# A two-layer sequence encoder on one core: which low parts a DMA forms, a fourth form of x made a chunk sooner, and one add from two neighbouring banks

## The chip, the cores and the metric

The kernel runs on one core of a Trainium2 chip. The metric is the device time of one execution in microseconds (us), lower is better. The core's engines run side by side and meet at semaphores: TensorE (PE in the profile, PEld for its loading of stationary operands), VectorE (DVE), ScalarE (ACT), GpSimd (POOL), SyncE (SP), and DMA queues that SP, POOL and ACT issue to. TensorE writes its products to PSUM, eight banks of 128 partitions x 512 floats; VectorE and ScalarE read them there.

## The reference

Two layers over 512 frames of width 1024, float32. Each layer has two half-step SwiGLU feed-forwards around a mixer (an mLSTM in layer 0, a gMLP in layer 1), then a gated input embedding, and each residual ends in a LayerNorm:

```python
def swiglu_ffn(x, w_gu, w_d):                     # hidden width 2816
    g, u = jnp.split(x @ w_gu, 2, axis=-1)
    return (jax.nn.silu(g) * u) @ w_d

for i in range(2):
    x = layer_norm(alpha*x + 0.5*swiglu_ffn(x, ffn1_wgu[i], ffn1_wd[i]), ...)
    x = layer_norm(alpha*x + mixer_i(x), ...)     # mLSTM (i = 0), gMLP (i = 1)
    x = layer_norm(alpha*x + 0.5*swiglu_ffn(x, ffn2_wgu[i], ffn2_wd[i]), ...)
    x = layer_norm(alpha*x + sigmoid(x @ ple_wg[i] + ple_bg[i]) * (p[i] @ ple_wp[i]), ...)
```

The change touches the feed-forwards. There are four of them; they are called first to fourth below, in order of time.

## The kernel before, in words

**Two parts for one number.** Each operand of a product is split into a high part (a copy in a rounded format, ScalarE) and a low part (what the copy lost). `mm3` multiplies high by high, high by low and low by high, so a block costs three matmuls (L353, L354, L355). The low part of a weight is formed by VectorE as source minus high part (L251, or L257 where it is put off), or by ScalarE and a DMA: ScalarE writes the source times -1 as rounded (L248), and a DMA that POOL issues adds the source to it (L249).

**The weights' queue.** `Weights` keeps one list of everything that has to be split, in the order of use. `fill` goes down that list as long as slots are free (four `main` slots for most, two `rows` slots for the down products), `take` hands out the next pair of parts, `release` gives a slot back when its product is issued and fills again. Raw weights come by SP's queue into three buffers of 1 MB (`load`, L208); a buffer is used again when every part formed from it is done.

**Seven products for eight.** Blocks of a matrix product are computed as two by two blocks in seven products instead of eight, with sums formed beforehand. For the up projection (gate and value columns of the weights, `up_forms`) the weight sums are formed in place in the raw tiles: product 2's operand in a quarter of g (L141, L142), product 4's there again (L149, L150). Products are counted from 0; `UP_BY_DMA` lists those whose low part is formed by DMA, and so marked as formed as soon as the DMA is issued (`done`). Others, in these chunks, are put off (`apart`): their subtraction runs at the next `lows()`, and only then does the product count as formed. `form_ahead(3)` forms the sums of the next three entries ahead of their turn if what they need is formed.

**A feed-forward** (`ffn`) goes through the 22 hidden blocks in six chunks of 2, 4, 4, 4, 4, 4. Chunks 0 to 3 compute the hidden activations block by block (`up`, tile `fps`). Chunks 4 and 5 (`up_products`) compute two blocks, a pair, by seven products (`UpPair`, tile `ups`, right operands from `UpForms`), so 14 products to a chunk and two pairs. While chunk c computes its hidden blocks, the down projection of chunk c-1 runs between them, again by seven products (`Group`, tile `gps`); after each, `add` adds the result to x in SBUF. The last chunk's down projection is done by `down` at the end (tile `dps`), block of 128 rows by block, followed by the LayerNorm.

**x's forms.** `UpForms` computes the sums of x that stand to the right in the pair's products. Its `steps` are run two at a time in chunk 3, from product `FORM_AT` on; what must wait for chunk 4 (one form is written over x's own parts) stands in `last` and runs behind the given product of chunk 4. The seventh product of the first pair needs the fourth form, high part L1003 and low part L1008.

**Banks.** Four PSUM banks belong to the up products (`up_bank`), four to everything else (`dn_bank`): down products, x's transposes (`turn_x`, run by hooks while the first products of the next stage go on), the mixers' smaller products. `dn_bank` takes the bank that has been free longest. A group holds two banks for its even and two for its odd products; `unpin` gives them back after its last two adds, L727. `add` issues one VectorE instruction for each bank.

**What sets the order.** The program is written out by hand: each engine executes its instructions in the order in which the Python code issues them, and waits in that order.

Of the kernel before, what the change touches and what calls it, by code (L numbers as in the profile page):

```python
# [10 lines left out]
F32 = mybir.dt.float32  # L11
F32R = mybir.dt.float32r
AF = mybir.ActivationFunctionType
# [31 lines left out]
PLE_EXTRA = 3  # L45
UP_BY_DMA = (1, 2, 4)

# [275 lines left out]
def hybrid_trunk(ctx: ExitStack, tc, x, p, ln_g, ln_b, ffn1_wgu, ffn1_wd, ffn2_wgu, ffn2_wd,  # L323
# [20 lines left out]
    ps_up = ctx.enter_context(tc.tile_pool(name="ps_up", bufs=1, space=PSUM))  # L344
    ps_dn = ctx.enter_context(tc.tile_pool(name="ps_dn", bufs=1, space=PSUM))
    dram = ctx.enter_context(tc.tile_pool(name="dram", bufs=1, space=DRAM))
# [33 lines left out]

    dn_order, pinned = deque(range(4)), {}

    def dn_bank(name, pin=False):

        i = next(i for i in dn_order if i not in pinned.values())
        dn_order.remove(i)
        dn_order.append(i)
        bank = ps_dn.tile([P, 512], F32, name=name, tag=f"dn{i}")
        if pin:
            pinned[id(bank)] = i  # L390
        return bank

    def unpin(bank):
        i = pinned.pop(id(bank))
        dn_order.remove(i)
        dn_order.append(i)
# [40 lines left out]
    UP_FROM = 4  # L437
    FORM_AT = 3
    turn_p = []
# [424 lines left out]
    class Group:  # L864
# [58 lines left out]
        def product(self):  # L923
            r = self.next_product
            self.next_product += 1
            if len(self.ready) == 1:
                self.finish_form()
            w, f = W.take(), self.ready.popleft()
            if r < 2:
                self.banks.append([dn_bank("gps", True) for _ in range(2)])  # L930
            for e, ps in enumerate(self.banks[r % 2]):
                for k in range(self.half):
                    i, j = (e, k) if self.by_tokens else (k, e)
                    mm3(ps, [a[:, i, j * P:(j + 1) * P] for a in f], [a[:, k] for a in w],
                        k == 0 and r in (0, 1, 3), k == self.half - 1, r not in (0, 1, 3))

        def add(self):

            r = self.next_add
            if r == self.next_product:  # L940
                return
            self.next_add += 1
            i, j = self.TO[r]
            for e, ps in enumerate(self.banks[r % 2]):
                residual(2 * i + e, j, ps, r in self.first)
                if r >= 5:
                    unpin(ps)


    class UpForms:  # L950


        def __init__(self, pool, late):
# [37 lines left out]

            def t3_t2():
                split(*self.t3, b)
                vec.tensor_sub(f32r(self.t2, late, "wlo"), c, self.t2[0].bitcast(F32))

            def x21():
                for i, s in enumerate(halves):
                    joined(d[i], 1, 0, s)

            def t4():  # L1000
                for i, s in enumerate(halves):
                    vec.tensor_sub(d[i], d[i], c[:, s])
                    sca.activation(f32r(self.t4, pool, "f1")[:, s] if not i else self.t4[0][:, s], d[i], AF.Copy)  # L1003

# [4 lines left out]

            self.last = {0: t3_t2, 2: x21, 3: t4, 4: t4_low}  # L1010
            self.right = [self.quarter(0, 0), self.quarter(1, 0), self.t2, self.t1, self.t3,
# [57 lines left out]
    def ffn(layer, k, rows, late, prepare=None):  # L1069
        with stage_pool("forms", 2) as fpool, stage_pool("quarters", Q_BUFS) as qpool, \  # L1070
                stage_pool("hpool", 2) as hpool, stage_pool("tforms") as tpool:
            name = (layer, k)
            W.open_raw(name, qpool, Q_BUFS)
            banks = deque(up_staged((layer, k) == (0, 0)))

# [48 lines left out]
            for c, n in enumerate(FFN_CHUNKS):  # L1124
# [52 lines left out]
                if c == 0:  # L1177
                    run_affine()
            W.apart = False
            return down(hs, False, norm, lazy=layer == 0, defer=prepare is not None)  # L1180

# [675 lines left out]
    def warm(n):  # L1857

        ps = up_bank("warm")
        for _ in range(n):  # L1860
            nc.tensor.transpose(ps[:, :P], ident, ident)

    warm(16)
    turn_x(0)
# [14 lines left out]
    gmlp()  # L1879
    ffn_ple(1, True)  # L1880


# [25 lines left out]
```

## Time and profile before

| | us |
|---|---|
| time, median of 3 runs | 2288.68 (2285.99 to 2288.74) |
| time of the profiled execution | 2286.79 |
| its span, first to last instruction | 2285.1 |
| TensorE busy | 2214.1 (97%) |
| VectorE busy | 1711.5 (75%) |
| ScalarE busy | 1049.7 (46%) |
| GpSimd busy | 145.4 (6%) |
| granted TensorE clock, mean | 0.985 |

The four stages with `up_products` lie at about 213 to 349, 983 to 1121, 1409 to 1546 and 2052 to 2192 us. The profile tells for each engine how long it was busy, and for idle time what ended it (the releaser, named by engine, tile and line). Line numbers are those of the code above. A tile's name stands without its number; `x2` at the end of a timeline row means two instructions in a row. "PEclk" is the share of full clock speed that TensorE was granted.

### The profile page before, as it was taken

To read this page: it belongs to the slowest core of one execution; us is meant where nothing else is said; L and a number is where in the kernel's file an instruction comes from. 1 tells how busy PE (TensorE), PEld (TensorE's weight loads), DVE (VectorE), ACT (ScalarE), POOL (GpSimd) and SP (SyncE) were. 2 spreads that over 40 slices of the span, in tenths; PEclk is the share of its full clock that TensorE was granted. 3 is DMA by queue.
4 is the path that set the end of the run, shared out by engine and by line. 5 is a ranking of instruction groups with operands and counts; after the bars stand their busy time and mean duration, and the time that the engine had idled before them with its cause. 6 is when DMAs were issued, how large, how long until landed. Compare 5 with 4: busy or idle time off the path is not lost.

```text
span 2285.1 us, 29387 instructions
## 1 busy us (share of the span) xinstructions
PE 2214.1 (97%) x11669; PEld 1908.1 (84%) x11669; DVE 1711.5 (75%) x2468; ACT 1049.7 (46%) x1476; POOL 145.4 (6%) x183
## 2 busy tenths in 40 slices
PE   9999889999999999989899999889999999998898
PEld 8888888888888888889788888887888888888887
DVE  5668887776776776788786768777788767688887
ACT  4335556464646533355354335545345453345532
POOL 1000000111101000000000000000011100000000
PEclk9999999999999999999999999999999999999999
DMA  6324543466747443335432324543438733344441
GB/s 200 104 87 127 150 118 122 103 152 128 163 111 148 127 141 101 100 95 148 129 124 86 117 78 123 146 127 114 138 75 158 174 102 111 102 120 133 104 142 56
DMA packets 213233, 278.91 MB, mean 122 GB/s; under 512 B 6580, under 2 KB 161332, under 8 KB 213096
## 3 DMA queue, kind: packets, MB, share of 16 engines
q1 hardware_dynamic: 168080, 211.83, 28.8%
q0 software_dynamic: 38400, 50.52, 14.1%
q10 hardware_dynamic: 6616, 14.69, 2.0%
q8 instruction: 92, 1.51, 0.3%
q14 instruction: 45, 0.37, 0.1%
HBM read 224.58 MB, written 2.11 MB: 99 GB/s over the span
## 4 chain that ended last, share of the span: by engine, by line
PE 84%; DVE 9%; ACT 2%; DMA 2%; issue 2%; DVEq 0%; ACTq 0%; POOL 0%; POOLq 0%
PE fps L353 8%; PE fps L355 8%; PE fps L354 8%; PE gps L355 6%; PE gps L353 6%; PE gps L354 6%; DVE wlo L257 3%; PE ups L354 2%; PE ups L353 2%; PE ups L355 2%; PE dps L354 2%; PE dps L353 2%; PE dps L355 2%; DMA wlo<-wraw 2%; PE gups L353 1%
## 5 line engine op out<-in xcount | busy, mean ns | idle before, releaser
L242 ACT ACTIVATE whi<-wraw 128x1024 fp32r<-128x1024 f32 (+1 forms) x388 | 400.5, 1048 | 206.9 <-DVE wraw L142 64.3
L353 PE MATMUL fps<-xh,whi 128*128 128x512 f32 x800 | 311.4, 389 | 0.0
L354 PE MATMUL fps<-xl,whi 128*128 128x512 f32 x800 | 311.3, 389 | 0.0
L355 PE MATMUL fps<-xh,wlo 128*128 128x512 f32 x800 | 311.2, 389 | 0.0
L251 DVE TENSOR_TENSOR wlo<-wraw,whi 128x1024 fp32r<-128x1024 f32 (+1 forms) x210 | 252.4, 1217 | 48.0 <-ACT whi L242 47.2
L353 PE MATMUL gps<-whi,fhi 128*128 128x512 f32 x644 | 251.9, 391 | 0.0
L354 PE MATMUL gps<-wlo,fhi 128*128 128x512 f32 x644 | 251.6, 391 | 0.0
L355 PE MATMUL gps<-whi,flo 128*128 128x512 f32 x644 | 251.3, 390 | 0.0
L242 ACT ACTIVATE whi<-wquarter 128x1024 fp32r<-128x1024 f32 (+1 forms) x140 | 136.0, 971 | 221.5 <-PE gps L355 141.4
L251 DVE TENSOR_TENSOR wlo<-wquarter,whi 128x1024 fp32r<-128x1024 f32 (+1 forms) x92 | 97.7, 1062 | 160.8 <-ACT whi L242 160.8
L249 POOL DMA_DIRECT2D wlo<-wraw x96 | 100.7, 1049 | 1515.9 <-ACT wlo L248 1328.0
L727 DVE TENSOR_TENSOR xt<-xt,gps 128x512 f32<-128x512 f32 x302 | 193.9, 682 | 3.1 <-PE gps L355 2.8
L355 PEld LDWEIGHTS fps<-xh,wlo 128*128 128x128 f32 x800 | 150.1, 188 | 31.2
L353 PEld LDWEIGHTS fps<-xh,whi 128*128 128x128 f32 x800 | 150.2, 188 | 31.1
L354 PEld LDWEIGHTS fps<-xl,whi 128*128 128x128 f32 x800 | 150.2, 188 | 31.1
L353 PE MATMUL ups<-xh,whi 128*128 128x256 f32 x512 | 145.2, 284 | 0.0
L354 PE MATMUL ups<-xl,whi 128*128 128x256 f32 x512 | 145.0, 283 | 0.0
L355 PE MATMUL ups<-xh,wlo 128*128 128x256 f32 x512 | 145.0, 283 | 0.0
L355 PEld LDWEIGHTS gps<-whi,flo 128*128 128x128 f32 x644 | 120.9, 188 | 26.2
L905 ACT ACTIVATE fhi<-h 128x512 fp32r<-128x512 f32 (+1 forms) x140 | 81.0, 579 | 131.6 <-DVE h L1149 47.5
L353 PEld LDWEIGHTS gps<-whi,fhi 128*128 128x128 f32 x644 | 121.2, 188 | 23.9
L354 PEld LDWEIGHTS gps<-wlo,fhi 128*128 128x128 f32 x644 | 121.1, 188 | 23.7
(361 smaller groups left out, 5104.7 us busy)
## 6 DMA issues: line engine op xcount, KB each, us to landing
wraw<-in_ffn_wgu_dram SPq DMA_DIRECT2D x79, 1024.0 KB, 7.1
wlo<-wraw POOLq DMA_DIRECT2D x96, 512.0 KB, 5.2
wquarter<-in_ffn_wd_dram SPq DMA_DIRECT2D x64, 512.0 KB, 3.8
wraw<-in_ml_w_in_dram SPq DMA_DIRECT2D x24, 1024.0 KB, 5.6
wraw<-in_gm_w_in_dram SPq DMA_DIRECT2D x15, 1024.0 KB, 5.5
wraw<-in_ffn_wgu_dram SPq DMA_DIRECT2D x17, 512.0 KB, 5.0
wraw<-in_ffn_wd_dram SPq DMA_DIRECT2D x8, 1024.0 KB, 5.0
wraw<-in_ml_w_out_dram SPq DMA_DIRECT2D x8, 1024.0 KB, 4.9
```

Source lines behind the costliest of these rows:

```text
L242: self.nc.scalar.activation(hi[:, s], src[:, s], AF.Copy)
L249: self.nc.gpsimd.dma_start(lo[:, s], src[:, s], accum_op=OP.add)
L251: self.nc.vector.tensor_sub(lo[:, s], src[:, s], hi[:, s].bitcast(F32))
L257: self.nc.vector.tensor_sub(lo, src, hi.bitcast(F32))
L353: mm(ps, st[0], mv[0], start=start, stop=False, skip_group_check=more)
L354: mm(ps, st[0], mv[1], start=False, stop=False, skip_group_check=more)
L355: mm(ps, st[1], mv[0], start=False, stop=stop, skip_group_check=more)
L727: vec.tensor_add(dst, dst, ps)
L905: sca.activation(hi, src, AF.Copy)
```

## The change

It has three parts.

1. `UP_BY_DMA` becomes (1, 4, 5, 6): the low parts of a pair's weights for products 1, 4, 5 and 6 are formed by ScalarE and DMA, that of product 2 by VectorE.
2. `FORM_AT` becomes 2, and the sum for x's fourth form and its high part (`x21`, `t4`) move from chunk 4 to the steps of chunk 3; the low part runs behind product 3 of chunk 4 instead of product 4.
3. In the feed-forwards the four banks form two tiles of two neighbouring banks (`use_dn(2)`), and `add` adds both at once, 1024 numbers a partition. Before `down`, and outside the feed-forwards, there are four tiles of one bank (`use_dn(1)`). Each `use_dn` starts the order of the tiles anew from the first. A user of a single bank (`dn_bank`) in a feed-forward takes the first half of a tile of two.

```diff
-UP_BY_DMA = (1, 2, 4)
+UP_BY_DMA = (1, 4, 5, 6)
...
-    dn_order, pinned = deque(range(4)), {}
-
-    def dn_bank(name, pin=False):
+    dn_order, pinned, dn = deque(), {}, {}
+
+    def use_dn(width):
+
+        if dn:
+            assert not pinned
+            dn["context"].__exit__(None, None, None)
+        dn["context"] = tc.tile_pool(name=f"ps_dn{width}", bufs=1, space=PSUM, reuse_waits="tile")
+        dn["pool"], dn["width"] = dn["context"].__enter__(), width
+        dn_order.clear()
+        dn_order.extend(range(4 // width))
+
+    def dn_tile(name, pin=False):
 
         i = next(i for i in dn_order if i not in pinned.values())
         dn_order.remove(i)
         dn_order.append(i)
-        bank = ps_dn.tile([P, 512], F32, name=name, tag=f"dn{i}")
+        tile_i = dn["pool"].tile([P, dn["width"], 512], F32, name=name, tag=f"dn{i}")
         if pin:
-            pinned[id(bank)] = i
-        return bank
+            pinned[id(tile_i)] = i
+        return tile_i
+
+    def dn_bank(name):
+        return dn_tile(name)[:, 0]
...
-    FORM_AT = 3
+    FORM_AT = 2
...  (Group.product)
             if r < 2:
-                self.banks.append([dn_bank("gps", True) for _ in range(2)])
-            for e, ps in enumerate(self.banks[r % 2]):
+                self.banks.append([dn_tile("gps", True) for _ in range(2 // dn["width"])])
+            for e in range(2):
+                tiles = self.banks[r % 2]
+                ps = tiles[0][:, e] if len(tiles) == 1 else tiles[e][:, 0]
...  (Group.add)
-            for e, ps in enumerate(self.banks[r % 2]):
-                residual(2 * i + e, j, ps, r in self.first)
+            tiles = self.banks[r % 2]
+            for e, ps in enumerate(tiles):
+                n = 2 // len(tiles)
+                dst = xt[:, 2 * i + e:2 * i + e + n, j * 512:(j + 1) * 512]
+                if r in self.first:
+                    vec.scalar_tensor_tensor(dst, dst, ALPHA, ps, op0=OP.mult, op1=OP.add)
+                else:
+                    vec.tensor_add(dst, dst, ps)
                 if r >= 5:
                     unpin(ps)
...  (UpForms)
+            def x21():
+                for i, s in enumerate(halves):
+                    joined(d[i], 1, 0, s)
+
+            def t4():
+                hi = f32r(self.t4, pool, "f1")
+                for i, s in enumerate(halves):
+                    vec.tensor_sub(d[i], d[i], c[:, s])
+                    sca.activation(hi[:, s], d[i], AF.Copy)
...
-            self.last = {0: t3_t2, 2: x21, 3: t4, 4: t4_low}
+            self.steps += [x21, t4]
+            self.last = {0: t3_t2, 3: t4_low}
...  (ffn, ahead of its first product)
+            use_dn(2)
             banks = deque(up_staged((layer, k) == (0, 0)))
...  (ffn, at its end)
             W.apart = False
+            use_dn(1)
             return down(hs, False, norm, lazy=layer == 0, defer=prepare is not None)
```

`use_dn(1)` is also called once at the very beginning.

More of the change, by code (lines that the diff above doesn't have):

```diff
@@ L344, in hybrid_trunk @@
     ps_up = ctx.enter_context(tc.tile_pool(name="ps_up", bufs=1, space=PSUM))
-    ps_dn = ctx.enter_context(tc.tile_pool(name="ps_dn", bufs=1, space=PSUM))
     dram = ctx.enter_context(tc.tile_pool(name="dram", bufs=1, space=DRAM))
@@ L387, in dn_bank, with unpin @@
         dn_order.append(i)
-        bank = ps_dn.tile([P, 512], F32, name=name, tag=f"dn{i}")
+        tile_i = dn["pool"].tile([P, dn["width"], 512], F32, name=name, tag=f"dn{i}")
         if pin:
-            pinned[id(bank)] = i
-        return bank
-    def unpin(bank):
-        i = pinned.pop(id(bank))
+            pinned[id(tile_i)] = i
+        return tile_i
+    def dn_bank(name):
+        return dn_tile(name)[:, 0]
+    def unpin(tile_i):
+        i = pinned.pop(id(tile_i))
         dn_order.remove(i)
@@ L990, in __init__ @@
             d = [tmp.tile([P, 2, 256], F32, name="x_d", tag="pad", bufs=3) for _ in range(2)]
-            def t3_t2():
-                split(*self.t3, b)
-                vec.tensor_sub(f32r(self.t2, late, "wlo"), c, self.t2[0].bitcast(F32))
             def x21():
@@ L1000, in t4, with t3_t2 @@
             def t4():
+                hi = f32r(self.t4, pool, "f1")
                 for i, s in enumerate(halves):
                     vec.tensor_sub(d[i], d[i], c[:, s])
-                    sca.activation(f32r(self.t4, pool, "f1")[:, s] if not i else self.t4[0][:, s], d[i], AF.Copy)
+                    sca.activation(hi[:, s], d[i], AF.Copy)
+            def t3_t2():
+                split(*self.t3, b)
+                vec.tensor_sub(f32r(self.t2, late, "wlo"), c, self.t2[0].bitcast(F32))
             def t4_low():
@@ L1861, in warm @@
             nc.tensor.transpose(ps[:, :P], ident, ident)
+    use_dn(1)
     warm(16)
@@ L1880, in hybrid_trunk @@
     ffn_ple(1, True)
+    dn["context"].__exit__(None, None, None)
 _INS = ['x', 'p', 'ln_g', 'ln_b', 'ffn1_wgu', 'ffn1_wd', 'ffn2_wgu', 'ffn2_wd',
```

## The prediction

> **What bounds the kernel now.** I read the busy times first, then TensorE's own list of waits, then the granted clock behind the longest waits, and last the timelines of VectorE, ScalarE and TensorE around them.
>
> ```profile
> span 2285.1 us, 29387 instructions
> PE 2214.1 (97%) x11669; PEld 1908.1 (84%) x11669; DVE 1711.5 (75%) x2468; ACT 1049.7 (46%) x1476; POOL 145.4 (6%) x183
> ```
>
> TensorE is busy 97% of the span; 71.0 us are left idle. Whatever else the change does to the other engines, it can give back only that idle time and what the clock loses behind it. The waits of TensorE say where it lies:
>
> ```profile
> PE ups L353 <- ACT us L1045: 28.4, 4, 8.1
> PE ups L354 <- DVE t_f L1008: 23.1, 4, 5.8
> PE dps L353 <- DVE xt L727: 4.3, 2, 2.2
> ```
>
> 51.5 us of it stand in two rows, four waits in each: one of either kind in every feed-forward, all in the stage with the products of pairs (`up_products`). Call them A (L1008, the low part of x's fourth form, 5.8 us each) and B (L1045, the first copy of a pair's bank, 6.6 to 8.1 us). Behind each the clock is down; the rows are six-microsecond stretches that begin where the eight waits end, the granted clock being the third figure from the right (0.65, 0.73, ...):
>
> ```profile
> 245.20:251.20 6.00, 6.00 (x34) 6.00 (x35) 4.64 (x5) 2.94 (x4) 0.64 (x1) 0.65 0.49 127
> 324.70:330.70 6.00, 5.98 (x31) 5.69 (x32) 6.00 (x8) 6.00 (x8) 0.85 (x1) 0.73 0.45 86
> 1015.50:1021.50 6.00, 6.00 (x30) 6.00 (x31) 4.63 (x5) 2.95 (x4) 0.65 (x1) 0.56 0.51 127
> 1095.70:1101.70 6.00, 6.00 (x31) 5.74 (x32) 6.00 (x8) 6.00 (x8) 0.84 (x1) 0.70 0.47 90
> 1441.50:1447.50 6.00, 5.97 (x28) 5.97 (x29) 4.67 (x5) 2.91 (x4) 0.61 (x1) 0.50 0.48 126
> 1521.70:1527.70 6.00, 6.00 (x30) 5.79 (x31) 6.00 (x8) 5.73 (x8) 0.84 (x1) 0.64 0.46 87
> 2084.50:2090.50 6.00, 5.99 (x33) 5.99 (x34) 4.65 (x5) 2.93 (x4) 0.63 (x1) 0.61 0.48 125
> 2165.80:2171.80 6.00, 6.00 (x28) 5.88 (x29) 6.00 (x8) 5.25 (x8) 0.86 (x1) 0.56 0.46 87
> ```
>
> The shortfalls 0.35, 0.27, 0.44, 0.30, 0.50, 0.36, 0.39 and 0.44 of 6 us sum to 18.3 us, 2.3 us a wait. So A and B together cost 51.5 + 18.3 = 69.8 us.
>
> Why they are there, in the first feed-forward (start, duration, engine and line; idle time before it in brackets):
>
> ```profile
> 231.11 1.29 DVE L964 TENSOR_TENSOR x_d<-xh,xl 128x512 f32<-128x512 f32 x2
> 235.85 1.29 DVE L1002 TENSOR_TENSOR x_d<-x_d,x_f 128x512 f32<-128x512 f32 x2
> 244.46 1.29 DVE L1008 TENSOR_TENSOR t_f<-x_d,t_f 128x512 fp32r<-128x512 f32 x2
> 255.17 1.23 DVE L150 TENSOR_TENSOR wraw<-wraw 128x1024 f32<-128x1024 f32 x1 [5.30 <-DMA wlo<-wraw]
> 317.56 1.23 DVE L150 TENSOR_TENSOR wraw<-wraw 128x1024 f32<-128x1024 f32 x1 [5.32 <-DMA wlo<-wraw]
> 319.90 0.69 DVE L1064 SCALAR_TENSOR_TENSOR us<-us 128x512 f32<-128x512 f32 x1
> 324.09 0.58 ACT L1045 ACTIVATE us<-ups 128x512 f32<-128x512 f32 x1
> 324.72 0.58 PE L353 MATMUL ups<-t_whi,whi 128*128 128x256 f32 x1 [6.75 <-ACT us L1045]
> ```
>
> ```profile
> 211.00:235.00 24.00, 24.00 (x171) 22.59 (x170) 22.27 (x26) 11.06 (x14) 0.83 (x1) 1.00 0.35 85
> DVE wraw L150 <- DMA wlo<-wraw: 54.5, 12, 5.4
> ```
>
> Wait A: VectorE (third busy figure: 22.27 of 24 us) is behind, and the low part at 244.46 stands in its queue after everything else of that stretch. Wait B: L150 overwrites the quarter of the weights that the DMA of product 2's low part still reads (products count from 0), and VectorE stands still for it, 5.3 us at a time, 54.5 us in twelve places. Then `gated` (L1064) is late, ScalarE's splits of it are late, and the copy of the next pair's bank, queued behind them on ScalarE, releases TensorE at 324.7.
>
> **The change part by part.**
>
> *Low parts of products 1, 4, 5, 6 by DMA instead of 1, 2, 4.* Sixteen pairs. Product 2's low part comes onto VectorE, those of 5 and 6 leave it: 16 subtractions fewer there, 16 more scaled copies on ScalarE, 16 more issues on POOL. What matters is the order: L150 now follows a VectorE instruction of its own queue, so the 54.5 us of standing still go. As product 2 counts as formed only when its low part has run, L149 and L150 are issued one product later, behind `gated`.
>
> ```profile
> 1122.18 6.90 DVE L257 TENSOR_TENSOR wlo<-wraw,whi 128x1024 fp32r<-128x1024 f32 x6 [1.30 <-ACT whi L242]
> 303.53 1.04 ACT L248 ACTIVATE wlo<-wraw 128x1024 fp32r<-128x1024 f32 x1
> wraw<-in_ffn_wgu_dram SPq DMA_DIRECT2D x79, 1024.0 KB, 7.1
> DMA to landing us min/median/max: 4.5/5.2/14.3
> ```
>
> A low part is 6.90/6 = 1.15 us. Wait B: without the 5.3 us and the low parts of products 5 and 6 (2.3 us), L1064 comes by 312.3 instead of 319.9; from there to the end of L1045 it is 4.8 us, 317.1; TensorE wants the bank at 324.72 - 6.75 = 318.0. With L149 and L150 (2.4 us) behind `gated` as well, some 3 us are to spare: B goes. The product that needs L150's result has 11.5 us of work ahead of its weights (4 to L150's end, two passes of ScalarE 2.0, 0.3 to POOL, 5.2 landing); TensorE has four products of 24 matmuls and two down products of 12 before it, 120 x 24/171 = 16.8 us by the row of 171 matmuls in 24 us.
>
> For the low parts now by DMA the path from a freed slot is 2.0 + 0.3 + 5.2 = 7.5 us; until use there are three products and two down products, 96 matmuls, 13.5 us. So they land 6.0 us early: cost 0 under that cover. On SP the next pair's load of 1 MB (7.1 us) is now behind product 5's DMA instead of a VectorE instruction, and lands about 14.6 us after the slot came free, 2.8 us after VectorE reaches L141 (84 matmuls, 11.8 us); the bank's copies and adds queued behind it on VectorE have a few us of slack. POOL's queue holds nothing but these issues there; ScalarE, 46% busy, hides its copies. For all of this I put 3 us (nothing at one end, and one of the two waits staying, 36.6 us for B with its clock, at the other); the lower end is nearer, as the covers above are.
>
> *x's fourth form a chunk sooner.* `FORM_AT` 2 instead of 3 moves every step one product sooner; L964's pair (1.29 us), L1002's pair (1.29) and the fourth form's high part on ScalarE go into the chunk before, to the place that the splits of t1 leave, and its low part one product sooner, to where L1002 stood. It issues no DMA. Without these 2.6 us and two low parts it starts at about 235.85 - 1.29 - 2.3 = 232.3; TensorE needs it at 245.2 - 5.8 = 239.4. A goes, with 7 us to spare.
>
> *One add from two banks.*
>
> ```profile
> L727 DVE TENSOR_TENSOR xt<-xt,gps 128x512 f32<-128x512 f32 x302 | 193.9, 682 | 3.1 <-PE gps L355 2.8
> ```
>
> The feed-forwards' 280 adds of 0.68 us become 140 of twice the size: one start saved each, next to nothing (two in a row last 1.28 us in the rows below, one instruction over 1024 numbers 1.23, as L150). VectorE is off the path there, so 0.
>
> *The banks.* This speaks against the change. `use_dn` starts the order anew, and two banks are now one tile. In a feed-forward the five groups take the two tiles in turns; four hooks before them (an even number) leave the order as it was, so in the second, third and fourth the last group's seventh product sits in tile 0. In the first, a fifth use (`colps`) shifts it to tile 1. `use_dn(1)` then gives the closing `down` banks 0 and 1, which are tile 0: its first row block must wait for the last add, while before it took the banks free longest and only the second block met that add.
>
> ```profile
> 1128.99 1.28 DVE L727 TENSOR_TENSOR xt<-xt,gps 128x512 f32<-128x512 f32 x2
> 1128.92 0.39 PE L353 MATMUL dps<-whi,wquarter 128*128 128x512 f32 x1
> 1130.28 0.39 PE L353 MATMUL dps<-whi,wquarter 128*128 128x512 f32 x1
> 1553.28 1.28 DVE L727 TENSOR_TENSOR xt<-xt,gps 128x512 f32<-128x512 f32 x2
> 1554.02 0.50 PE L353 MATMUL dps<-whi,wquarter 128*128 128x512 f32 x1 [2.16 <-DVE xt L727]
> 2199.83 1.28 DVE L727 TENSOR_TENSOR xt<-xt,gps 128x512 f32<-128x512 f32 x2
> 2201.30 0.39 PE L353 MATMUL dps<-whi,wquarter 128*128 128x512 f32 x1
> ```
>
> The add is late by itself (it is behind five or six low parts on VectorE, the row at 1122.18, which wait for slots that the last product frees), so a faster VectorE does not help. The second block starts at 1130.28, 1554.02 and 2201.30 now. Then the first block would start at the add's end (1130.2, 1554.5, 2201.0), run 24 matmuls of (1130.28 - 1128.92)/6 = 0.227 us, 5.4 us, and lose 2.3 us of clock as after the eight waits: second block at 1137.9, 1562.2, 2208.7. That is 7.6 + 8.2 + 7.4 = 23.2 us more.
>
> Entering a feed-forward, the hooks that turn x take tile 0 and then tile 1:
>
> ```profile
> 782.89 0.60 PE L595 MATMUL xps<-ident,xt 128*128 128x128 f32 x4
> 783.81 0.67 DVE L727 TENSOR_TENSOR xt<-xt,dps 128x512 f32<-128x512 f32 x1
> 1849.46 0.60 PE L595 MATMUL xps<-ident,xt 128*128 128x128 f32 x4
> 1852.76 0.67 DVE L727 TENSOR_TENSOR xt<-xt,dps 128x512 f32<-128x512 f32 x1
> ```
>
> In the second feed-forward the second hook (782.89) must now wait for the mixer's last add (784.48): 1.6 us. In the fourth, the gMLP's `down` ends in banks 0 and 1 (its single banks are taken in multiples of four but for the two of the last spatial product), so the first hook (1849.46) waits until 1853.43: 4.0 us, and between 0 and 2.3 of clock, of which I take 1. Together 6.6.
>
> **Sum:** -51.5 - 18.3 + 23.2 + 6.6 + 3 = -37.0 us. Against the profiled span 2285.1 that is 2248; that execution's time, 2286.79, stands 1.9 below the median 2288.68, so the median becomes 2251.
>
> The Trainium skill, "TensorE: Matmul & The Clock Gate", Part 1, "What's actually happening", says that the clock halves after an idle window and comes back after one busy window of about 3.4 us. By that a long wait would cost 1.7 us of clock; with eight waits gone and three come the estimate from the page is 2255. The rows behind the waits (2.3 us each) decide for the sum above.
>
> **The rivals.**
>
> *No bank waits.* If the tiles lie otherwise than I read them, the 29.8 us of the last two parts do not come: 2222. For it: the whole of them is argued from the order of the code; against it: the order can be followed step by step.
>
> *One wait stays in part.* VectorE, standing at L141 for the load that is now behind a DMA, may keep `gated` late. B whole would give 2251 + 36.6 - 3 = 2285, half of it about 2268. For it: the load's 7.1 us begin only when a DMA has landed; against it: 3 us of margin for B, 7 for A.
>
> *Slower: weights late by DMA.* TensorE waits for no low part by DMA now. Four of seven go that way after, three in consecutive products (4, 5, 6), beside SP's loads. A landing takes 4.5 to 14.3 us; above 13.5 - 2.3 = 11.2 us TensorE waits, and above 12.4 us (1.2 us more at each of the 32 products) the gain is gone. At 14.3 us it would be 32 x 3.1 = 99 us, 2350. Against it: the landing that VectorE waited for at L150, in the chain of waits, took 4.51 us from its issue.
>
> ```profile
> 312.93 4.51 DMA wlo<-wraw
> ```
>
> The Trainium skill, "DMA: Bandwidth & Descriptors", "Issuing engines are not separate DMA queues", says that transfers from SP and POOL run on the same 16 engines and interleave, which is how this would come about; the median row, 5.2 us, does not bear out so much of it.
>
> **How the numbers follow.** The forecast, 2251 (2240 to 2262 by the bounds of clock and loads), 0.56; no bank waits 0.15; a wait that stays 0.20, of which 0.04 near 2285; late weights 0.09. The range 2218 to 2276 leaves out the last case and the upper end of the third, 0.16. About 0.2%, 4.6 us, is what a measurement can tell: faster 0.56 + 0.15 + 0.16 = 0.87, same 0.04, slower 0.09.
>
> **What would show it.** After the change L1008 and L1045 are gone from TensorE's waits; L150 waits for no DMA; new rows "dps L353 <- DVE xt" of some 8 us stand in the second to fourth feed-forward and "xps <- DVE xt" at the start of the second and fourth; the first keeps its 2.2 us. Waits of `ups` on a DMA, or `dps` without its 8 us, would prove me wrong.

## The result: 8 us faster, where 37 were forecast

The changed kernel takes 2279.11 us (median of 8 runs, 2272.96 to 2285.07) against 2287.25 (8 runs, 2284.43 to 2288.74) for the kernel before: ratio 0.9966, 95% interval 0.9953 to 0.9979. The page of the changed kernel begins:

```profile
span 2277.8 us, 29282 instructions
PE 2209.0 (97%) x11669; PEld 1897.9 (83%) x11669; DVE 1687.2 (74%) x2312; ACT 1059.9 (47%) x1492; POOL 158.9 (7%) x199
```

TensorE's list of waits after the change (engine, tile and line that waited, what ended the wait; us in total, times, longest):

```profile
PE dps L352 <- DVE xt L965: 32.1, 4, 9.4
PE ups L352 <- ACT us L1067: 12.9, 12, 2.5
PE xps L607 <- DVE xt L739: 5.3, 2, 3.8
PE ups L353 <- DVE t_wlo L1024: 4.6, 4, 1.1
PE ups L354 <- DMA wlo<-wraw: 2.3, 2, 1.4
```

Wait A (on x's fourth form) is gone, and wait B is gone as one long wait in each feed-forward; twelve short ones on the same copy (L1067 now) and four on `t_wlo` stand in their place. The first row of a `down` waits 32.1 us in four places, of which three are the bank waits that were forecast.

Matmul by matmul (both profiled executions have 11669 in the same order, so the start of each can be set against the other) they differ so:

| term | forecast, us | measured, us |
|---|---|---|
| A, B and their clock | -69.8 | -67.2 (A 33.4, B 33.8) |
| late loads, fuller ScalarE: the rest of the product stages | +3 | +22.9 |
| starts of `down` | +23.2 (0, 7.6, 8.2, 7.4) | +29.5 (4.8, 7.7, 8.6, 8.4) |
| hooks at the starts of feed-forwards | +6.6 | +7.0 (1.9 and 5.1) |
| sum | -37.0 | -7.8 (the spans: -7.3) |

Where the first row ends and the second begins is a choice: counted from two matmuls before each wait to 36 behind it, A and B give 69.9 and the second row about 26; the sum of the two hardly changes.

The start of the second `down` in the changed kernel, by the timelines of VectorE and TensorE:

```profile
1110.07 6.90 DVE L257 TENSOR_TENSOR wlo<-wraw,whi 128x1024 fp32r<-128x1024 f32 x6 [1.30 <-ACT whi L242]
1116.89 1.21 DVE L965 TENSOR_TENSOR xt<-xt,gps 128x1024 f32<-128x1024 f32 x1
```

```profile
1118.25 0.77 PE L352 MATMUL dps<-whi,wquarter 128*128 128x512 f32 x1 [9.35 <-DVE xt L965]
```

Six low parts for the next stage stand ahead of the last group's add; TensorE's first matmul of `down` waits for its end, 9.35 us. Behind this wait and its two sisters the granted clock (third figure from the right) is down as it was behind A and B, by 0.38, 0.25 and 0.49 of 6 us, 2.2 us a time:

```profile
1118.20:1124.20 6.00, 5.95 (x17) 4.75 (x18) 0.00 (x0) 0.00 (x0) 0.00 (x0) 0.62 0.72 263
1539.60:1545.60 6.00, 6.00 (x20) 4.83 (x21) 0.00 (x0) 0.00 (x0) 0.00 (x0) 0.75 0.32 123
2185.30:2191.30 6.00, 6.00 (x15) 4.70 (x15) 0.00 (x0) 0.00 (x0) 0.00 (x0) 0.51 0.72 259
```

### The profile page after: what moved, and what is told of

It is laid out like the page before. It is cut to its first block, busy times and chain, and to the rows that moved or that the text cites. A ratio compares the mean times of both kernels' runs of the same rounds, so it can differ in the third digit from the quotient of the medians.

```text
span 2277.8 us, 29282 instructions
## 1 busy us (share of the span) xinstructions
PE 2209.0 (97%) x11669; PEld 1897.9 (83%) x11669; DVE 1687.2 (74%) x2312; ACT 1059.9 (47%) x1492; POOL 158.9 (7%) x199
## 5 line engine op out<-in xcount | busy, mean ns | idle before, releaser
L251 DVE TENSOR_TENSOR wlo<-wraw,whi 128x1024 fp32r<-128x1024 f32 (+1 forms) x214 | 257.1, 1216 | 49.9 <-ACT whi L242 49.1
L249 POOL DMA_DIRECT2D wlo<-wraw x112 | 114.2, 1020 | 1507.0 <-ACT wlo L248 1294.7
L965 DVE TENSOR_TENSOR xt<-xt,gps 128x1024 f32<-128x1024 f32 (+1 forms) x178 | 185.1, 1052 | 1.2 <-PE gps L354 1.2
L352 PE MATMUL ups<-xh,whi 128*128 128x256 f32 x512 | 146.2, 286 | 12.9 <-ACT us L1067 12.9
```

The lines of the kernel that those rows point to most:

```text
L249: self.nc.gpsimd.dma_start(lo[:, s], src[:, s], accum_op=OP.add)
L251: self.nc.vector.tensor_sub(lo[:, s], src[:, s], hi[:, s].bitcast(F32))
L352: mm(ps, st[0], mv[0], start=start, stop=False, skip_group_check=more)
L965: vec.tensor_add(dst, dst, ps)
```

## The experiments

All times are medians; each ratio is to the kernel before, run beside it on the same chip, with its 95% interval.

**The parts one by one.** `b_dma` is the kernel before with part 1, `b_form` with part 2, `b_dma_form` with both, `b_banks` with part 3.

```diff
b_dma:       -UP_BY_DMA = (1, 2, 4)   +UP_BY_DMA = (1, 4, 5, 6)
b_form:      -FORM_AT = 3             +FORM_AT = 2
             -self.last = {0: t3_t2, 2: x21, 3: t4, 4: t4_low}
             +self.steps += [x21, t4]; self.last = {0: t3_t2, 3: t4_low}
b_banks:     the third part's lines of the change, with before's UP_BY_DMA, FORM_AT and UpForms
```

> The kernel before, with the first part alone: low parts 1, 4, 5 and 6 by DMA, the third on VectorE; x's fourth form and the banks as before. Theory 1: the stand of VectorE behind the third low part's DMA (5.3 us at the add of line 150) is what made both of TensorE's waits in the product stage (on x's fourth form, 33.4 us with the low clock over four feed-forwards, and on ScalarE's copy, 33.8); both go with this part alone, and the small new losses in the stage (22.5 us) come with it: 2243 us. Rival: the wait on x's fourth form goes only with its earlier place (the second part), and half or more of the 33.4 us stays: 2260 to 2277 us; its lines show TensorE waiting at t_f.

> The kernel before with the second part alone: x's fourth form a chunk sooner; low parts 1, 2 and 4 by DMA and the banks as before. Theory 1: the wait on t_f (23.3 us in 4, 33.4 with the clock) goes with this part alone, the wait on ScalarE's copy (28.4 us in 4, 33.8 with the clock) stays since VectorE still stands behind the third low part's DMA, and a wait on t_wlo of some 8 us with its clock comes: about 2262 us. Rival: the fourth form was late only through VectorE's stand at line 150, so that its earlier place is worth no more here than on top of the first part (6 us by the medians): 2275 to 2283 us.

> The kernel before, with the first two parts: low parts 1, 4, 5 and 6 by DMA, and x's fourth form a chunk sooner; the banks and the adds as before. Theory 1: the changed kernel's losses at the starts of `down` and at the hooks (29.5 + 7.0 us) are the banks' alone; without them the product stages keep their gain of 44 us: 2243 us. Rival: the one add of 1.21 us for two of 0.68 us and its banks, free at once, helped the product stage; without them VectorE is later there and part of the 44 us is lost again: 2255 to 2270 us.

> The kernel before, with the third part alone: pairs of neighbouring banks, one add to x from both, tile 0 first; low parts 1, 2 and 4 by DMA and x's fourth form as before. Theory 1: the starts of the second to fourth `down` lose 23 to 25 us, the hooks 7, nothing is won: 2315 us. Rival: the adds, which cost VectorE 0.15 us less in each of 7 products of 64 groups and free both banks at once, shorten the waits of the product stage, so that it comes out at 2300 us or less.

| | us | ratio |
|---|---|---|
| part 1 | 2252.48 | 0.9847 (0.9833 to 0.9860) |
| part 2 | 2273.33 | 0.9938 (0.9926 to 0.9951) |
| parts 1 and 2 | 2246.17 | 0.9823 (0.9805 to 0.9841) |
| part 3 | 2319.48 | 1.0140 (1.0126 to 1.0154) |
| all three | 2279.11 | 0.9966 (0.9953 to 0.9979) |

Part 3 costs 33 us, alone (2319.48 against 2286.29) as on top of the others (2279.11 against 2246.17). Theory 1 holds for it: nothing is won by the one add. Its waits, alone:

```profile
PE dps L352 <- DVE xt L965: 29.6, 4, 9.4
PE ups L352 <- ACT us L1065: 29.1, 5, 7.9
PE ups L353 <- DVE t_f L1028: 23.3, 4, 5.8
```

A and B are untouched and the `down` starts stand on top. The next fences are TensorE's waits in `b_dma`, in `b_form` and in `b_dma_form`. Part 1 alone takes B away, and A only in part: the rival's row is there, 17.8 us where it was 23.1, and the time, 2252, lies between its two expectations (2243; 2260 to 2277). The short waits are not there (19.4 us is all that `ups` and `gps` wait). Part 2 alone takes A away, leaves B, and brings a wait of its own on `wlo`; both expectations for it missed, 13.5 us being won where 25 or 4 to 12 were expected. With both parts the time is near theory 1's 2243, and neither A nor B is left, but short waits are (the row on `t_wlo` stands in neither of the two single runs):

```profile
PE ups L354 <- DVE t_f L1008: 17.8, 4, 4.5
```

```profile
PE ups L353 <- ACT us L1047: 28.9, 8, 7.9
PE gps L354 <- DVE wlo L257: 9.5, 4, 2.4
```

```profile
PE ups L353 <- ACT us L1047: 9.4, 11, 1.8
PE ups L354 <- DVE t_wlo L1004: 5.1, 4, 1.3
PE ups L355 <- DMA wlo<-wraw: 1.4, 2, 0.8
```

So parts 1 and 2 win 40 us where the steps for them said 66.8, and part 3 costs 33 where they said 29.8.

**The banks.**

```diff
 a_order (in the changed kernel's use_dn):
-        dn_order.extend(range(4 // width))
+        # banks: the old dn_order, in single banks
+        dn_order.extend(sorted(range(4 // width), key=lambda i: max(banks.index(i * width + e) for e in range(width))))
 a_place: the same, and ahead of it
+        for i in range(4 // width):
+            dn["pool"].tile([P, width, 512], F32, name="place", tag=f"dn{i}")
```

> The changed kernel, with one edit: when the banks are opened anew, the tile that was freed longest ago is taken first, instead of tile 0 (`down` then begins on the banks of the next to last product, and the hooks at the start of a feed-forward on the tile whose last reader is oldest). Theory 1, the order of the banks: the four starts of `down` lost 4.8, 7.7, 8.6 and 8.4 us against the kernel before and the hooks 1.9 and 5.1; the starts of the second to fourth give back 20 to 25 us with the low clock behind them, the hooks some 5 to 7, and the time is about 2250 us. Rival: the start of `down` is late since the last group's add itself comes late on VectorE (in the first feed-forward the start is on the other tile and lost 4.8 all the same); then the wait moves to the second row block and no more than 8 us come back, 2271 us or more.

Measured 2279.08 us, 0.9960 (0.9947 to 0.9973): as the changed kernel, with the same waits.

```profile
PE dps L352 <- DVE xt L967: 32.1, 4, 9.4
```

Neither theory was tried by it: in the built program the first row block of the second `down` still lies in bank 4, where the last product lay. A pool lays out its tiles in the order in which they are first asked for, so taking tile "dn2" first only gives that name to the first banks. With the tiles placed first:

> The changed kernel, taking the tile freed longest ago first, and now with the tiles placed in fixed order when the banks are opened: the run before it of the same name order left every matrix product on the banks it had been on, since a reopened set of banks lays out its tiles in the order in which they are first asked for, whatever they are called. Theory 1, the banks of the first row block: at the starts of the second to fourth `down` the wait of 9.35, 8.96 and 9.35 us shrinks to what the kernel with the first two parts alone shows there (1.2, 2.75 and 1.2 us), the first start stays (4.4 us); with the clock behind them 24 to 30 us, and 3 to 6 us at the hooks: 2246 to 2253 us. Rival: the second row block then meets the late add and the wait is only moved by a row block of 5.5 us or less: 2262 to 2270 us.

Measured 2249.47 us, 0.9843 (0.9825 to 0.9861): theory 1. The waits at the four starts are now 4.5, 1.2 and 1.3 (first and second block), 3.9 and 1.2 us; the rows, with the hooks' behind them:

```profile
PE dps L352 <- DVE xt L969: 9.7, 3, 4.5
PE dps L352 <- ACT whi L242: 2.4, 2, 1.2
PE xps L611 <- DVE xt L743: 3.0, 2, 1.5
```

Of part 3's 33 us, 30 were the order of the tiles. The pair of banks is not to blame as such, but neither does its one add win anything (2249.47 against 2246.17 without it, intervals overlapping).

**Which low parts go by DMA, and the order of the forms.** All from `b_dma_form`.

```diff
f_146, f_145, f_14, f_4: UP_BY_DMA = (1, 4, 6), (1, 4, 5), (1, 4), (4,)
f_t4: -self.steps += [x21, t4]; self.last = {0: t3_t2, 3: t4_low}
      +self.steps += [x21];     self.last = {0: t3_t2, 1: t4, 3: t4_low}
a_place_14: a_place with UP_BY_DMA = (1, 4)
```

> The kernel before with the first two parts, but the sixth low part back on VectorE: low parts 1, 4 and 6 by DMA. Theory 2, the late load: the sixth low part's DMA has to land before the next u can be loaded into that buffer, and VectorE stands for it at line 141 (19.7 us in 5 stands); with the part on VectorE these stands fall below 5 us, TensorE's waits on ScalarE's copy of the up banks (9.4 us in 11) and half of the small losses go, and the time is 2234 to 2240 us against 2246. Rival: VectorE's 16 more passes of 1.22 us (19.5 us, in stages where it is full) make the same products late by as much or more: 2246 to 2256 us, with the stands at line 141 gone but TensorE's waits still there.

> The kernel before with the first two parts, but the seventh low part back on VectorE: low parts 1, 4 and 5 by DMA. Theory 4, ScalarE's passes: with four low parts by DMA ScalarE has 16 more negated copies of 1.05 us than with three, and the copies of the up banks behind them make TensorE wait (9.4 us in 11; with 1, 4 and 6 it was 2.3 in 4, but there the seventh part's DMA came late, 16.6 us in 21); without a DMA for the seventh neither wait is there, and the time is 2234 to 2241 us. Rival: VectorE, which has 16 passes of 1.22 us more, is late with the seventh part in the place of the DMA, and TensorE waits on wlo from VectorE 10 us or more: 2246 to 2256 us.

> The kernel before with the first two parts, but two low parts by DMA only, 1 and 4; the fifth, sixth and seventh in order on the engines as their kinds have it, the sixth and seventh on VectorE. Theory 4, ScalarE's passes: with 32 negated copies of 1.05 us fewer ScalarE is never late, TensorE's waits on its copies go (9.4 us in 11), and with one DMA fewer each pair nothing else comes late: 2236 to 2244 us. Rival: VectorE with 32 passes of 1.22 us more (39 us) becomes the late one: TensorE waits on adds, low parts or gated products of VectorE by 20 us or more over four feed-forwards, 2260 us or more.

> The kernel before with the first two parts, but one low part by DMA only, the fifth product's (4). Theory 5, each DMA'd low part that TensorE meets early is late: with 1 and 4 by DMA TensorE waits 9.1 us in 12 for the second part's DMA; on VectorE these go, VectorE is still under full (126.3 of 140 us in the first feed-forward's product stage, 16 passes of 1.22 us over four stages add 4.9 to each), and the time is 2234 to 2240 us. Rival: with 131 of 140 us VectorE is the late engine, every take and add comes later, and TensorE's waits on VectorE and ScalarE's copies rise by 10 us or more: 2248 us or more.

> The kernel before with the first two parts, but the subtraction and the high part of x's fourth form put after the second product of the chunk (x21 stays a chunk sooner). Theory 3, order on VectorE: in the second part the 2.5 us of x's fourth form stand ahead of the third form's low part, so that TensorE waits for t_wlo (5.1 us in 4, and 8.2 us with the low clock behind them over four feed-forwards); with the fourth form behind it this wait goes and the wait on t_f (17.8 us in 4 without the second part) does not come back: 2237 to 2241 us. Rival: the fourth form is late again, TensorE waits at t_f as long as t_wlo was before, and nothing is won: 2245 to 2252 us.

> The changed kernel with the tiles taken in the order in which they came free and placed in fixed order, and low parts 1 and 4 alone by DMA. Theory 6, the one add is worth something only where VectorE is short: with two low parts by DMA VectorE is busy 126.3 of 140 us in the first product stage, one add of 1.21 us in place of two that take 1.28 us then shortens waits, and the time is 2236 to 2241 us against 2243 with two adds. Rival: the bank pairs, freed together by one add at its end, cost the starts of `down` and the hooks 3 us as they did with four parts by DMA (2249.5 against 2246.2 us): 2244 to 2250 us.

| low parts by DMA | us | ratio | waits of `ups` and `gps`, us |
|---|---|---|---|
| 1, 4, 5, 6 (`b_dma_form`) | 2246.17 | 0.9823 (0.9805 to 0.9841) | 16.4 |
| 1, 4, 6 | 2248.97 | 0.9834 (0.9820 to 0.9848) | 24.0 |
| 1, 4, 5 | 2252.28 | 0.9843 (0.9830 to 0.9856) | 24.9 |
| 1, 4 | 2243.01 | 0.9805 (0.9792 to 0.9818) | 18.8 |
| 4 | 2249.32 | 0.9837 (0.9823 to 0.9851) | 19.4 |
| 1, 4, 5, 6, `t4` later (`f_t4`) | 2249.86 | 0.9840 (0.9827 to 0.9854) | 19.7 |
| 1, 4, with pairs of banks (`a_place_14`) | 2244.71 | 0.9818 (0.9803 to 0.9833) | 15.5 |

Theory 4 had the time of `f_14` right but not its rows (3.0 us of waits on the copy stay and 9.1 on DMAs come), and missed for `f_145`; theories 2, 3 and 5 missed in time. Where a rival's time came (2, 3, 4 for `f_145`, 5) its rows did not, or only in part; `a_place_14` came out as its rival, though its interval overlaps that of `f_14`. Whoever forms the low parts, 15 to 25 us of short waits are left, only under other names. TensorE's rows with 1, 4, 6:

```profile
PE ups L355 <- DMA wlo<-wraw: 16.6, 21, 1.7
PE ups L353 <- ACT us L1047: 2.3, 4, 1.3
```

with 1, 4, 5:

```profile
PE ups L353 <- ACT us L1047: 17.1, 20, 1.8
```

and with `t4` later, where the wait on `t_wlo` did go:

```profile
PE ups L353 <- ACT us L1047: 17.8, 11, 2.5
```

`f_146` was to take away VectorE's stands at L141 (its waits there for the next raw weights), and did not: they are 23.8 us in 4, where `b_dma_form` has 19.7 in 5.

```profile
DVE wraw L141 <- DMA wraw<-in_ffn_wgu_dram: 23.8, 4, 7.9
```

The load is issued sooner, but VectorE is released no sooner (at 272.05 us against 271.67). SP's queue in `b_dma_form` and `f_146`:

```profile
265.78 27.00 SPq L208 DMA_DIRECT2D wraw<-in_ffn_wgu_dram  x3
```

```profile
261.43 33.31 SPq L208 DMA_DIRECT2D wraw<-in_ffn_wgu_dram  x3
```

So `f_146` does not clear the late load, the rival that I had named; the traces show it at work. In the first feed-forward of the changed kernel VectorE stands 7.0 us at L141, is busy without a break until its next `us` (L1070), ScalarE has waited for that, and the copy of the bank behind it releases TensorE:

```profile
273.98 1.23 DVE L141 TENSOR_TENSOR wraw<-wraw 128x1024 f32<-128x1024 f32 x1 [7.00 <-DMA wraw<-in_ffn_wgu_dram]
291.15 0.68 DVE L1070 TENSOR_TENSOR us<-us,ups 128x512 f32<-128x512 f32 x1
291.86 0.63 ACT L1081 ACTIVATE us<-us 128x512 f32<-128x512 f32 x1 [3.03 <-DVE us L1070]
293.87 0.58 ACT L1067 ACTIVATE us<-ups 128x512 f32<-128x512 f32 x1
294.50 0.39 PE L352 MATMUL ups<-xh,whi 128*128 128x256 f32 x1 [2.52 <-ACT us L1067]
```

The same 20.5 to 20.7 us lie between stand and wait in the other feed-forwards and runs, and it is the longer stands that have the waits:

| | stands of over 1 us at L141, us | TensorE's wait on the copy that far behind each |
|---|---|---|
| changed kernel | 7.0, 7.5, 5.4, 5.1 | 2.5, 1.8, 1.3, 0.9 |
| `f_145` | 5.2, 5.3, 5.3, 5.1 | 1.1, 1.4, 1.4, 1.3 |
| `b_dma_form` | 4.6, 4.4, 4.6, 5.9 | 0.6, none, 0.6, 1.8 |
| `x_plain` (below) | 3.0, 3.0, 3.4, 3.3 | none |
| `b_dma` | 2.7, 3.4, 2.3, 4.2 | none |
| `f_14` | 1.9, 2.7, 2.5, 2.6 | none |

In `f_146`, where TensorE waits 16.6 us for DMAs besides, only the longest, 7.9 us, has one (1.3 us). The changed kernel's other waits on the copy have another cause. Ahead of them ScalarE is not idle but busy without a break, with two passes for low parts (L248) in its last 5.5 us:

```profile
319.56 1.04 ACT L248 ACTIVATE wlo<-wraw 128x1024 fp32r<-128x1024 f32 x1
322.92 1.04 ACT L248 ACTIVATE wlo<-wraw 128x1024 fp32r<-128x1024 f32 x1
324.39 0.57 ACT L1067 ACTIVATE us<-ups 128x512 f32<-128x512 f32 x1
325.02 0.39 PE L352 MATMUL ups<-xh,whi 128*128 128x256 f32 x1 [1.49 <-ACT us L1067]
```

Of the changed kernel's 12.9 us on the copy, four waits (6.6 us) stand behind the stands and eight (6.3 us) behind such passes.

**Whose work makes the short waits.** All from `b_dma_form`; all but the last leave work out, as their expectations say, so they are no kernels to use.

```diff
x_adds (Group.add):  +if r in (0, 1, 5, 6) or not W.apart:
                          residual(2 * i + e, j, ps, r in self.first)
x_neg (fill):  -nc.scalar.activation(lo[:, s], src[:, s], AF.Copy, scale=-1.0)
               -nc.gpsimd.dma_start(lo[:, s], src[:, s], accum_op=OP.add)
               +nc.gpsimd.dma_start(lo[:, s], src[:, s].bitcast(F32R))
x_both: both;  x_plain: x_neg with the activation kept
p_neg:  the activation's work as nc.gpsimd.tensor_scalar_mul(lo[:, s], hi[:, s], -1.0), accumulation kept
```

> The kernel before with the first two parts, which in the stages with products of pairs leaves out the adds to x of the third, fourth and fifth product of a group (its output lacks these terms). VectorE loses three of seven pairs of adds there, some 5 to 8 us of its 117 in the first feed-forward's product stage. Theory 7, VectorE's load: the small waits of TensorE (16.4 us in rows, about 19 with the clock) are made by VectorE being late; at least half of them go and the time is 2232 to 2238 us against 2246. Rival 1, ScalarE's negated copies: nothing changes, 2243 to 2248 us. Rival 2, the chain from bank to bank is too long by itself, whatever the load: also 2243 to 2248 us, but then x_neg changes nothing either.

> The kernel before with the first two parts, in which the four low parts by DMA are plain copies of the source, without ScalarE's negated copy ahead of them and without accumulation (so these low parts hold the whole value; TensorE's work is as before). ScalarE loses 64 passes of 1.05 us in the four product stages, 16.8 of its 82 us in the first, and the DMAs start about 1 us sooner. Theory 7, VectorE's load: TensorE's waits on ScalarE's copies stay in the main, 2241 to 2246 us. Rival 1, ScalarE's negated copies: the waits on its copies of the up banks (9.4 us in 11) go, VectorE's waits on fhi (96.8 us in 79) fall below 70, and the time is 2230 to 2238 us.

> Both of the last two edits in one kernel: three of seven adds to x left out in the product stages, and the low parts by DMA as plain copies without ScalarE's pass. Theory 7 and rival 1: no less than the better of the two alone, and if each engine covers for the other, clearly more: 2226 to 2232 us, with TensorE's waits in the product stages below 5 us. Rival 2, the chain from bank to bank is too long by itself: 2240 us or more.

> The kernel before with the first two parts, ScalarE's negated copies kept, but the DMA of the low parts a plain copy instead of an accumulating one (so these low parts hold the whole value). Theory 8, ScalarE's passes: the waits of TensorE on its copies of the up banks stay (9.4 us in 11), and the time is 2240 us or more. Rival, the DMA itself: the shorter landing (4.0 us in place of 5.8) frees the weights' buffers sooner, VectorE's stands at line 141 (19.7 us in 5) fall below 6 us with TensorE's waits behind them, and the time is 2230 us or less.

> The kernel before with the first two parts, in which POOL makes the negated copy (of the high part, so the sum of the DMA is the same) in place of ScalarE; nothing is left out. POOL is busy 7% of the span, and no row shows what such a pass of 128x1024 numbers takes on it. Theory 8, ScalarE's passes: if POOL takes no more than 2 us for one, ScalarE is 16.8 us per product stage lighter, TensorE's waits on its copies go, and the time is 2225 to 2236 us, of which late low parts take what the longer chain costs. Rival, the DMA itself: nothing of this helps, 2243 to 2250 us; and if a pass on POOL takes 4 us or more, its queue of four in a pair (one pair takes about 31 us) makes low parts late, with TensorE's waits on the DMA of low parts in the rows: 2255 us or more.

| | us | ratio | `ups`, `gps` waits, us |
|---|---|---|---|
| `b_dma_form` | 2246.17 | 0.9823 (0.9805 to 0.9841) | 16.4 |
| `x_adds` | 2247.41 | 0.9825 (0.9811 to 0.9838) | 17.0 |
| `x_plain` | 2235.59 | 0.9777 (0.9762 to 0.9791) | 14.8 |
| `x_neg` | 2220.09 | 0.9703 (0.9690 to 0.9716) | 1.4 |
| `x_both` | 2218.27 | 0.9699 (0.9685 to 0.9712) | 1.4 |
| `p_neg` | 2318.45 | 1.0138 (1.0121 to 1.0155) | 56.2 |

The product stage of the first feed-forward (busy us of TensorE, its loading, VectorE, ScalarE, POOL) in `b_dma_form`, `x_adds` and `x_neg`:

```profile
205.00:345.00 140.00, 134.17 (x900) 122.89 (x898) 117.05 (x140) 82.23 (x103) 12.64 (x15) 1.00 0.59 150
```

```profile
205.00:345.00 140.00, 134.24 (x901) 122.92 (x899) 110.08 (x129) 82.04 (x103) 12.64 (x15) 1.00 0.59 149
```

```profile
205.00:345.00 140.00, 137.50 (x916) 126.66 (x915) 121.87 (x149) 68.66 (x88) 8.50 (x16) 0.99 0.47 158
```

VectorE is the fuller engine, 117 of 140 us, but 7 us less on it (second row) change nothing: theory 7 falls. The lateness of VectorE in the table above comes from its stands, not from how full it is. 13.6 us less on ScalarE, which is busy 82, put TensorE from 134 to 137.5 and take the short waits away. What is left of them in `x_neg`:

```profile
PE ups L353 <- DVE t_wlo L1003: 1.4, 4, 0.3
```

`x_plain` divides it: without the accumulation alone 10.6 us go by the medians (6.9 between the profiled executions), and the other 15.5 with the passes, whose absence also lets the DMAs start about 1 us sooner. Both theories of `x_plain` were half right, and its rows say by what: the stands shrink and the waits behind them go, the waits behind the passes stay (6.5 us in 8, as in `b_dma_form`). The stands in `b_dma_form`, `x_plain` and `x_neg`, and the copy's row in `x_plain`:

```profile
DVE wraw L141 <- DMA wraw<-in_ffn_wgu_dram: 19.7, 5, 5.9
DVE wraw L141 <- DMA wraw<-in_ffn_wgu_dram: 12.8, 4, 3.4
DVE wraw L141 <- DMA wraw<-in_ffn_wgu_dram: 3.9, 3, 1.6
```

```profile
PE ups L353 <- ACT us L1047: 6.5, 8, 1.5
```

Nearly all that `x_plain` and `x_neg` win lies in the four product stages and the starts of `down` behind them; the 48 low parts that go by DMA in other stages moved the start of no later stage by over 1 us. The DMA of a low part with and without accumulation, by the page's list of DMA issues (KB, median us to landing), in `b_dma_form` and `x_plain`:

```profile
wlo<-wraw POOLq DMA_DIRECT2D x112, 512.0 KB, 5.8
```

```profile
wlo<-wraw POOLq DMA_DIRECT2D x112, 512.0 KB, 3.8
```

`p_neg` lies between its two conditions, 3.11 us for a pass on POOL (group row: count, busy us, mean ns), and goes the way of the second: low parts come late.

```profile
L248 POOL TENSOR_SCALAR wlo<-whi 128x1024 fp32r<-128x1024 f32 x112 | 348.4, 3111 | 1217.5 <-ACT whi L242 1130.6 <-DVE wquarter L111 86.6
```

```profile
PE ups L355 <- DMA wlo<-wraw: 54.9, 21, 5.2
```

VectorE's timeline beside one such pass (POOL's, from 230.61 to 233.70):

```profile
230.30 2.20 DVE L908 TENSOR_TENSOR flo<-h,fhi 128x512 fp32r<-128x512 f32 x1
232.43 1.21 DVE L257 TENSOR_TENSOR wlo<-wquarter,whi 128x1024 fp32r<-128x1024 f32 x1
```

**The version to use** is the kernel before with parts 1 and 2 and low parts 1 and 4 by DMA (`f_14`): 2243.01 us, 0.9805 (0.9792 to 0.9818). It beats the changed kernel clearly, `b_dma_form` (0.9823) and `a_place_14` (0.9818) not beyond their intervals.

## Why the prediction was wrong

*A and B go: right.* 67.2 us with the clock against 69.8, and the runs of single parts give each to its part: B to part 1, A to part 2 with a small share of part 1. The clock was 2.0 us for each of these waits ((67.2 - 51.5)/8; 2.3 by the longer count), where I had 2.3; behind the three new ones it was 2.2, by the windows above. The Trainium skill's rule that I had set beside it ("TensorE: Matmul & The Clock Gate", Part 1, "What's actually happening": the clock comes back after a busy window of about 3.4 us, from which I had estimated 1.7 us) gives less than any of these.

*"For all of this I put 3 us": this step failed, by 20 us* (23 by the longer count). It was inside its own bounds (0 to 36.6 us), and I had taken the lower end. The 22.9 us are short waits, 20.1 us of them in TensorE's list, and they have four sources.

- The late load, 6.6 us in four waits. I had it landing "2.8 us after VectorE reaches L141", with "a few us of slack" behind. VectorE stood there 5.1 to 7.5 us. A few us of slack there were: in the runs of the table above, stands of up to 4.4 us cost nothing, longer ones did. In the first feed-forward SP issues the load at 266.0 us, VectorE reaches L141 at 267.0 and is released at 274.0.
- ScalarE's passes, 6.3 us in eight waits. "ScalarE, 46% busy, hides its copies" takes the mean over the span; in the product stage ScalarE is busy 82 of 140 us, and in its order the two passes stand ahead of the copies that free the up banks.
- `t_wlo`, 4.6 us in four waits. It belongs to the step on x's fourth form, which had no price for what stands behind the moved form. Neither part alone makes it: part 1 puts product 2's low part on VectorE ahead of it, part 2 the fourth form. `f_t4` takes the wait away and gets longer ones on the copy instead.
- Low parts by DMA, 2.3 us in two waits, which I had landing 6.0 us early. A last 0.3 us are on two low parts of VectorE.

`x_neg` shows what they have in common: without the passes and the accumulation the stands are 3.9 us, 1.4 us of short waits are left, and the first two parts give 2220 us, 67 less than the kernel before. That the prediction's steps for them had said 66.8 is in part luck, since `x_neg` also leaves out the passes that the kernel before has. The short waits could not be seen in the trace of before, where A and B held TensorE back 5.8 and 7.1 us a time and the rest had that much slack: `b_dma` has the same passes and DMAs, and as long as A stands there (4.5 us a time) the short waits are 1.6 us in all.

*`down` starts: right in kind and place, 29.5 for 23.2.* The three bank waits measured 24.7 by the matmuls' starts, 1.5 more than forecast. The other 4.8 is the first feed-forward, of which I had said that "the first keeps its 2.2 us": the wait became 4.4. TensorE gets there 9.4 us earlier than before (at 345.0 us for 354.4), the add that it waits for, behind the next stage's low parts, only 7.1 us (wait over at 349.4 for 356.6). `b_dma_form`, without any pairs of banks, waits 3.98 us at that place.

*Hooks: right,* 7.0 for 6.6. *The adds: right,* 0: `x_adds` shows that even leaving three of seven out in the product stages is worth nothing.

*The rivals.* "One wait stays in part" (2268 to 2285) is the one that holds the measured time. Its mechanism, VectorE standing at L141 for the load, is there, but it gives 6.6 us of short waits and no long one; that the sum comes into its range is luck. "Weights late by DMA" did not come with the change (2.3 us in 2), though it does with another choice of low parts (`f_146`, 16.6 us in 21). Of what was to be seen, L1045 did not leave TensorE's list, it fell from 28.4 to 12.9 us (L1067 in the changed kernel).

What stays open: why `f_145`, with one pass fewer a pair, waits longer on the copy (17.1 us in 20; 11.8 of them not behind a stand), and `f_146` shorter (2.3). How the 15.5 us between `x_plain` and `x_neg` divide between ScalarE's time and the DMA's earlier start, with the shorter stands behind it, was not tried apart either.

## What to carry to other kernels

When the long waits of the bounding engine go, price the short ones behind them: take each helper's busy time in that stage and its order there, not its share of the span, and ask which queue has the added work ahead of what the bounding engine waits for. Follow a helper's stand forward to the place where the bounding engine meets it, and ask how much of it the slack covers; an edit that was to remove a stand has tested nothing while the stand is still in the trace. A reopened set of PSUM tiles is a new order: say which bank the last reader still holds, and look at the built addresses, not at the tiles' names. Run each part of a change alone before judging the sum; here two parts won 40 us and the third gave 33 of them back.

## What was not expected of the hardware

A pass over 128x1024 floats that takes 1.04 us on ScalarE takes 3.11 us on POOL, and a VectorE subtraction beside it 2.20 us instead of 0.69 (the row at 230.30 of `p_neg`). The Trainium skill, "SBUF — State Buffer", "Who interferes with whom", says that VectorE and GpSimd share one pair of ports as an exclusive lock. That row agrees; the next, beside the same pass, does not show it (1.21 us, as without POOL). Of the VectorE instructions that meet such a pass, 59 of 253 with two inputs in SBUF last over 30% longer than the same line does in `b_dma_form`, and none of the 149 that use a PSUM tile. An accumulating DMA of 512 KB between SBUF tiles lands 2 us later than a plain one (medians of 5.8 and 3.8 us), and its issue holds POOL 1.02 instead of 0.62 us (means of 112 in `b_dma_form` and `x_plain`).
